# Queries and keys stored doubled and interleaved, loaded over 128 partitions; VectorE and GpSimd operations kept apart by the planner; down projection prepared five pairs ahead

## The chip, the cores and the metric

One core of a Trainium2 chip. The metric is the device time of one execution in microseconds (us); for the kernel before it is the median of three runs. PE is TensorE, DVE VectorE, ACT ScalarE, POOL GpSimd; SP issues DMAs, and so does ACT here.

## The reference

A decoder block on `x` of 1 x 1024 x 1024 in float32. One projection of the normed input gives a pooling branch, the queries and keys of four heads of differential attention, values and two gates; the gated sum of the two branches is projected and added, and a SwiGLU network of hidden width 2816 follows. Cut to what the change touches:

```python
z = einsum('bsd,de->bse', rms_norm(h, mix_pre_g), w_in)      # p, q, k, v, gate_a, gate_b
ya = einsum(pool_mixer(p), w_branch_a)
# 4 heads; each has two query halves and two key halves of width 64
a  = softmax(q1 k1' * scale + bias) - lam * softmax(q2 k2' * scale + bias)   # causal
yb = einsum(rms_norm(a @ v, subln_g) * (1 - lambda_init), w_branch_b)
m  = sigmoid(gate_a) * ya + sigmoid(gate_b) * yb
h  = h + rms_norm(m @ w_out, mix_post_g)
u  = rms_norm(h, ffn_pre_g)
f  = silu(u @ w_ffn_gate) * (u @ w_ffn_up)
h  = h + rms_norm(f @ w_ffn_down, ffn_post_g)
```

## The kernel before, in words

Every float32 operand is split into a high part (rounded to a shorter float32, type fp32r) and a low part (what is left), and a product of blocks is three matmuls: L799 (high by high), L800 and L801 (low by high, high by low). The large products run as units of seven half-size products (`seven_steps`, L824), accumulated in banks named Y, Z and X. In `seven_steps` the first product of a unit is copied out of Y by ACT (`p1`, L835), and the third product then goes on adding into the same bank Y; it can start only when that copy is done.

Stages by their time in the trace:
- 0 to 40 us: norm of the input and transposes.
- 40 to 112 us: queries and keys of the four heads. `qk_done` (L871) scales and splits each 128 x 512 result into a staging tile `qk_st` of high and low part and stores it into `qkd[h][e]` in device memory (e is 0 for queries, 1 for keys). The stores are issued on ACT's queue, by `store()` (L1040) for the first head and directly (L881) for the others.
- 112 to 327 us: values, pooling branch and gates. `load_head0` (L1192) loads head 0's tiles `K` and `QA` near the end.
- 327 to 527 us: `mixer` (L232), attention of 32 blocks of rows and both branch projections. Its order on every engine is written by a planner, the class `Plan` (L73): each step is a task with an engine, a cost, what it reads and writes and a rank; `schedule` (L142) runs a model of the engines, of the tile slots and of the DMA (`DMA_LATENCY`, `DMA_RATE`, L51) and fixes the order, which is emitted as it stands. At run time nothing of the planner's clock is left, only the order and the waits for data and for slots.
- 527 to 630 us: output projection (`out_matmul`, `out_norm`).
- 630 to 960 us: gate and up projections of the network; 960 to 1255 us: the down projection, L1430 to L1590. Outside the planned stages a general scheduler of the language arranges the engines' instructions.

In the mixer a head needs three tiles of 128 partitions x 2 x 1024. For each of the head's two maps m, `K` holds the key half's high part in one 64-partition half and its low part in the other; `QA` holds the query's high part in both halves and `QB` its low part in both halves. A score block is then two accumulated matmuls, `QA` by `K` and `QB` by `K`, and wants all three. The kernel before fills each tile with four DMAs of 64 partitions x 4 KB (256 KB each), so twelve for a head: `load_qk` (L343) issues those of `K` and `QA`, `load_bv` (L354) those of `QB` and then the one of the values `V`. SP issues all of them, in the planner's order (`dma`, L340).

The mixer's elementwise steps that matter here: `branch_weights` (L378) loads a 128 x 1024 weight block, casts it on ACT (L383) and forms the low part `wb_lo`, on POOL for the pooling branch (L385, weights against their high part) and on DVE for the attention branch (L655 by `k.sub`). `scores` (L423) ends with a scaled sum of the two maps (E, DVE, L465). `head_norm` (L516) computes 1/rms per row on POOL (`rstd`, a power, L522) and multiplies the head's output with it on DVE (`O` by `rstd`, issued by the helper `tt`, L257). The transposed attention block `AT` is split by ACT and DVE (low part at L655), and PE then multiplies it with `V`.

The down projection works through 77 pairs (a block of the hidden layer and a block of its weights): `load_s` (L1459) loads two pairs' worth of hidden blocks `s_raw`, `operands` (L1467) splits both into `s_op` and `w_op` on ACT (L732) and DVE (L655), `down_block` does 12 matmuls. The loop prepares pair n + DEPTH before the matmuls of pair n, and fetches `s_raw` of pair n + DEPTH + 3. In the last product, `residual` (L1510) loads the rows to be added (`hr`), and `finish` (L1515) adds and stores them.

## Time and profile before

| | us |
|---|---|
| median of three runs | 1266.66 |
| the three runs | 1263.72, 1266.66, 1266.82 |
| the profiled execution | 1262.81 |
| its span (first to last instruction) | 1261.0 |

The views used below come from the profiled execution; their times count from the span's start. A line of the waits says which engine, doing what, waited for whom, and then the total in us, how often, and the longest. A line of a timeline says start, duration, engine, line, operation, output and inputs, with the idle time before it and who ended that in brackets. A line of the windows says from:to, length, the busy time of each engine with its count, the clock that PE was granted (1.00 is full), the share of the DMA engines' time and the GB/s.

### The profile page before, as it was taken

How to read it: one execution, taken by the hardware profiler on the slowest of the kernel's cores; microseconds unless marked ns; L12 is line 12 of the kernel's file. 1: busy time of each engine (PE TensorE's matmuls, PEld its weight loads, DVE VectorE, ACT ScalarE, POOL GpSimd, SP SyncE). 2: the span in 40 equal slices, each digit the busy share in tenths (PEclk: the TensorE clock that was granted, in tenths of full speed). 3: DMA queues.
4: the chain of work that ended last, by engine and by line, in shares of the span. 5: the costliest groups of instructions: out<-in, count | busy, mean ns of one | idle time of the engine just before them, and what ended most of it. 6: DMA issues, size and time to landing. Idle time of an engine off the chain costs nothing.

```text
span 1261.0 us, 15705 instructions
## 1 busy us (share of the span) xinstructions
PE 1244.0 (99%) x5912; PEld 1042.4 (83%) x5912; DVE 837.3 (66%) x1296; ACT 581.2 (46%) x1039; POOL 144.0 (11%) x128
## 2 busy tenths in 40 slices
PE   8999999999999999999999999999999999999997
PEld 8888888888888998888888888888888888888886
DVE  5985785535589998755697645645645547965666
ACT  7553344434567874344553333333333333554542
POOL 4100000000201100010102111111111012000221
PEclk9999999999999999999999999999999999999999
DMA  8363338323797128423314332223322367733336
GB/s 254 114 192 131 136 123 246 112 92 117 242 272 186 52 69 283 150 101 118 117 59 126 125 107 102 92 94 108 125 100 96 115 212 276 244 102 100 90 94 209
DMA packets 135453, 179.15 MB, mean 142 GB/s; under 512 B 7633, under 2 KB 90321, under 8 KB 132945
## 3 DMA queue, kind: packets, MB, share of 16 engines
q1 hardware_dynamic: 124832, 147.61, 37.7%
q10 hardware_dynamic: 10544, 30.54, 6.3%
q8 instruction: 46, 0.75, 0.3%
q14 instruction: 31, 0.25, 0.1%
HBM read 124.39 MB, written 53.74 MB: 141 GB/s over the span
## 4 chain that ended last, share of the span: by engine, by line
PE 89%; DMA 3%; DVE 3%; issue 2%; ACT 1%; POOL 1%; SPq 0%; POOLq 0%; DVEq 0%; ACTq 0%
PE Y L799 10%; PE Y L800 10%; PE Y L801 10%; PE X L799 5%; PE X L801 5%; PE X L800 5%; PE Yd L800 3%; PE Z L801 3%; PE Z L800 3%; PE Yd L801 3%; PE Z L799 3%; PE Yd L799 3%; PE o L254 2%; PE branch L799 2%; PE branch L800 2%; PE branch L801 2%
## 5 line engine op out<-in xcount | busy, mean ns | idle before, releaser
L728 DVE TENSOR_TENSOR p<-Z,p 128x512 f32<-128x512 f32 x34 | 23.5, 691 | 162.8 <-PE Z L801 154.0
L800 PE MATMUL Y<-A_lo,Wh 128*128 128x512 f32 x296 | 115.4, 390 | 0.3 <-DVE A_lo L655 0.3
L799 PE MATMUL Y<-A_hi,Wh 128*128 128x512 f32 x296 | 115.3, 390 | 0.0
L801 PE MATMUL Y<-A_hi,Wl 128*128 128x512 f32 x296 | 115.2, 389 | 0.0
L799 PE MATMUL X<-S_hi,Wh 128*128 128x512 f32 x280 | 109.2, 390 | 0.0
L799 PE MATMUL Y<-S_hi,Wh 128*128 128x512 f32 x280 | 109.2, 390 | 0.0
L801 PE MATMUL Y<-S_hi,Wl 128*128 128x512 f32 x280 | 109.1, 389 | 0.0
L800 PE MATMUL Y<-S_lo,Wh 128*128 128x512 f32 x280 | 109.0, 389 | 0.0
L800 PE MATMUL X<-S_lo,Wh 128*128 128x512 f32 x280 | 108.9, 389 | 0.0
L801 PE MATMUL X<-S_hi,Wl 128*128 128x512 f32 x280 | 108.9, 389 | 0.0
L768 ACT CAST Wh<-wf_t 128x1024 fp32r<-128x1024 f32 x70 | 72.9, 1055 | 72.1 <-PE X L800 30.6
L768 ACT CAST Wh<-w_raw 128x1024 fp32r<-128x1024 f32 x72 | 60.7, 844 | 66.0 <-PE Z L800 39.9
L655 DVE TENSOR_TENSOR Wl<-wf_t,Wh 128x1024 fp32r<-128x1024 f32 x70 | 87.1, 1251 | 5.1 <-ACT Wh L768 5.1
L655 DVE TENSOR_TENSOR w_op<-wd,w_op 128x512 fp32r<-128x512 f32 x77 | 56.4, 732 | 49.8 <-ACT w_op L732 49.8
L732 ACT CAST w_op<-wd 128x512 fp32r<-128x512 f32 x77 | 48.0, 623 | 73.2 <-PE Yd L801 30.7
L655 DVE TENSOR_TENSOR Wl<-w_raw,Wh 128x1024 fp32r<-128x1024 f32 x72 | 69.1, 960 | 13.9 <-ACT Wh L768 13.9
L799 PE MATMUL Yd<-w_op,s_op 128*128 128x512 f32 x176 | 68.7, 390 | 0.6 <-ACT w_op L732 0.6
L800 PE MATMUL Yd<-w_op,s_op 128*128 128x512 f32 x176 | 68.7, 390 | 0.3 <-DVE w_op L655 0.3
L801 PE MATMUL Yd<-w_op,s_op 128*128 128x512 f32 x176 | 68.3, 389 | 0.0
L728 DVE TENSOR_TENSOR wf_t<-w_raw,wf_t 128x512 f32<-128x512 f32 x70 | 65.7, 939 | 1.1
L800 PEld LDWEIGHTS Y<-A_lo,Wh 128*128 128x128 f32 x296 | 55.6, 188 | 12.1 <-DVE A_lo L655 0.7
L801 PEld LDWEIGHTS Y<-A_hi,Wl 128*128 128x128 f32 x296 | 55.6, 188 | 11.6
(274 smaller groups left out, 3063.1 us busy)
## 6 DMA issues: line engine op xcount, KB each, us to landing
s_raw<-fsd SPq DMA_DIRECT2D x35, 512.0 KB, 3.6
w_raw<-in_w_in_dram SPq DMA_DIRECT2D x32, 512.0 KB, 4.2
w_raw<-in_w_ffn_gate_dram SPq DMA_DIRECT2D x22, 512.0 KB, 3.9
w_raw<-in_w_ffn_up_dram SPq DMA_DIRECT2D x22, 512.0 KB, 3.8
fsd<-fss SPq DMA_DIRECT2D x11, 1024.0 KB, 3.9
wd<-in_w_ffn_down_dram SPq DMA_DIRECT2D x44, 256.0 KB, 5.6
fsd<-F SPq DMA_DIRECT2D x33, 256.0 KB, 2.3
qkd<-qk_st ACTq DMA_DIRECT2D x16, 512.0 KB, 3.8
```

The source lines that it names most:

```text
L254: nc.tensor.matmul(o, l, r, start=start, stop=stop, skip_group_check=skip)
L655: nc.vector.tensor_tensor(out=o, in0=a, in1=f32(hi), op=ALU.subtract)
L728: nc.vector.tensor_tensor(out=o, in0=a, in1=b, op=op)
L732: nc.scalar.copy(hi, a)
L768: nc.scalar.copy(hi, a)
L799: nc.tensor.matmul(o, ah, bh, start=start, stop=False, skip_group_check=goes_on)
L800: nc.tensor.matmul(o, ah, bl, start=False, stop=False, skip_group_check=goes_on)
L801: nc.tensor.matmul(o, al, bh, start=False, stop=stop, skip_group_check=goes_on)
```

## The change

Three edits.

First, the stores and loads of queries and keys. Instead of `qkd[h][e]` there are `qd[h][i]` (i = 0 the high parts of the queries, 1 the low parts) and `kd[h]`. Of the queries, each part is written twice next to itself: a store of one part of `qk_st`, broadcast over two copies. Of the keys, high and low part lie side by side in each row, as before. Read as rows (partition, copy), 64 partitions of the store give 128 rows, so a load of half a tile covers all 128 partitions with one DMA of 512 KB. A head takes six loads for twelve; a result of a query takes two stores of 512 KB for one. The 128 rows now alternate between high and low part (`K`) in place of lying in two blocks; `QA` and `QB` hold equal rows in pairs, so the sum over the partitions is the same.

Second, the planner. Its tasks get a flag `port`. Flagged DVE tasks (the `wb_lo` and output-weight low parts, E, `O` by `rstd`, two steps of the gated sum) are not started in the model while a flagged POOL task (`wb_lo` at L385, `rstd` at L522) runs, and the other way round. No instruction is added; the emitted order may differ. The two DMA constants of the model are changed as well.

Third, `DEPTH` in the down projection is 5 in place of 3.

```diff
-DMA_LATENCY, DMA_RATE = 2.2, 0.36
+DMA_LATENCY, DMA_RATE = 2.4, 0.38
...
+        t.port = port
...
-                    at = max(f, ready, self.room(t))
+                    at = max(f, ready, self.room(t), port["POOL" if e == "DVE" else "DVE"] if t.port else 0.0)
...
+            if t.port:
+                port[e] = t.end
...
+def interleaved(src, m):
+    return src[m * HD:(m + 1) * HD].rearrange("p i s -> (p i) s")
...
         for m in range(2):
-            r, r2 = hs[m], hs[1 - m]
-            dma(lambda m=m, r=r: f32(K()[r, m, :]), lambda r=r: k.qkd[h][1][r, 0, :], rank, 0.262, w=[(K, (m, 0))])
-            dma(lambda m=m, r=r2: f32(K()[r, m, :]), lambda r=r: k.qkd[h][1][r, 1, :], rank, 0.262, w=[(K, (m, 1))])
-            for rr in (r, r2):
-                dma(lambda m=m, rr=rr: f32(QA()[rr, m, :]), lambda r=r: k.qkd[h][0][r, 0, :], rank, 0.262,
-                    w=[(QA, (m, rr.start))])
+            dma(lambda m=m: f32(K()[:, m, :]), lambda m=m: interleaved(k.kd[h], m), rank, 0.524, w=[(K, m)])
+            dma(lambda m=m: f32(QA()[:, m, :]), lambda m=m: interleaved(k.qd[h][0], m), rank, 0.524, w=[(QA, m)])
...
         for m in range(2):
-            for rr in hs:
-                dma(lambda m=m, rr=rr: f32(QB()[rr, m, :]), lambda m=m: k.qkd[h][0][hs[m], 1, :], rank, 0.262,
-                    w=[(QB, (m, rr.start))])
+            dma(lambda m=m: f32(QB()[:, m, :]), lambda m=m: interleaved(k.qd[h][1], m), rank, 0.524, w=[(QB, m)])
...
-              r=[ms], w=[r], rank=rank)
+              r=[ms], w=[r], rank=rank, port=True)
...
-    qkd = [[dr.tile([P, 2, S], F32, name=name("qkd")) for _ in range(2)] for _ in range(NH)]
+    qd = [[dr.tile([P, 2, S], F32, name=name("qd")) for _ in range(2)] for _ in range(NH)]
+    kd = [dr.tile([P, 2, S], F32, name=name("kd")) for _ in range(NH)]
...
-        if stores is None:
-            nc.scalar.dma_start(qkd[h][e][:, :, half(t)], f32(st))
+        if e == 1:
+            out_ = [(kd[h][:, :, half(t)], f32(st))]
         else:
-            stores.append((qkd[h][e][:, :, half(t)], f32(st)))
+            out_ = [(qd[h][i][:, :, half(t)], f32(st[:, i:i + 1, :]).to_broadcast([P, 2, HALF])) for i in range(2)]
+        if stores is not None:
+            stores.extend(out_)
+            return
+        for o, s in out_:
+            nc.scalar.dma_start(o, s)
...
-            nc.sync.dma_start(f32(K[r, m, :]), qkd[0][1][r, 0, :])
-            nc.sync.dma_start(f32(K[r2, m, :]), qkd[0][1][r, 1, :])
-            for rr in (r, r2):
-                nc.sync.dma_start(f32(QA[rr, m, :]), qkd[0][0][r, 0, :])
+            nc.sync.dma_start(f32(K[:, m, :]), interleaved(kd[0], m))
+            nc.sync.dma_start(f32(QA[:, m, :]), interleaved(qd[0][0], m))
...
-    kept, loaded, DEPTH, SPLIT = {}, {}, 3, 6
+    kept, loaded, DEPTH, SPLIT = {}, {}, 5, 6
```

The flag `port=True` is set in the same way on the other steps named above.

More of the change, by code (lines that the diff above doesn't have):

```diff
@@ L92, in given, with op @@
         return s
-    def op(self, engine, cost, fn, r=(), w=(), rank=0.0, size=0.0, claim=(), chain=None, behind=None):
+    def op(self, engine, cost, fn, r=(), w=(), rank=0.0, size=0.0, claim=(), chain=None, behind=None,
+           port=False):
         t = Task(engine, cost, fn, rank, size)
+        t.port = port
         if behind is not None:
@@ L146, in schedule @@
         open_ = {e: [] for e in free}
-        dma_free, order = 0.0, []
+        dma_free, order, port = 0.0, [], {"DVE": 0.0, "POOL": 0.0}
         for t in self.tasks:
@@ L363, in load_bv @@
         return QB, Vt
-    hs = [slice(0, HD), slice(HD, P)]
     seq = [(h, qb) for h in range(NH) for qb in (QLAST if h == NH - 1 else QORDER)]
@@ L385, in branch_weights @@
             pl.op("POOL", 2.6, lambda: G.tensor_tensor(out=lo(), in0=raw(), in1=f32(hi()), op=ALU.subtract),
-                  r=[raw, hi], w=[lo], rank=rank)
+                  r=[raw, hi], w=[lo], rank=rank, port=True)
         else:
-            pl.op("DVE", 1.23, lambda: k.sub(lo(), raw(), hi()), r=[raw, hi], w=[lo], rank=rank)
+            pl.op("DVE", 1.23, lambda: k.sub(lo(), raw(), hi()), r=[raw, hi], w=[lo], rank=rank, port=True)
         return hi, lo
@@ L466, in scores @@
                                                                     in1=view[0](), op0=ALU.mult, op1=ALU.add),
-              r=[E[1], cf], w=[E[0]], rank=r0 + .3)
+              r=[E[1], cf], w=[E[0]], rank=r0 + .3, port=True)
         attends[h, qb] = E[0], view[0], rec
@@ L527, in fn @@
             tt(o, o, r().unsqueeze(2).to_broadcast([P, n, P]), ALU.mult)
-        pl.op("DVE", dve(n * P), fn, r=[r], w=[(O[h], q) for q in blocks], rank=rank)
+        pl.op("DVE", dve(n * P), fn, r=[r], w=[(O[h], q) for q in blocks], rank=rank, port=True)
     def turn_head(h, t, rank):
@@ L580, in mixer @@
         pl.op("DVE", dve(HALF), lambda m=m, c=c, sg=sg: tt(m()[:, c, :], m()[:, c, :], sg()[:, 0], ALU.mult),
-              r=[(sg, 0)], w=[(m, c)], rank=r0 + 2)
+              r=[(sg, 0)], w=[(m, c)], rank=r0 + 2, port=True)
         if (1, d) in (k.unfinished if k else [(1, 6), (1, 7)]):
@@ L588, in mixer @@
         pl.op("DVE", dve(HALF), lambda m=m, c=c, sg=sg: tt(m()[:, c, :], m()[:, c, :], sg()[:, 1], ALU.add),
-              r=[(sg, 1)], w=[(m, c)], rank=r0 + 1)
+              r=[(sg, 1)], w=[(m, c)], rank=r0 + 1, port=True)
     wo = []
@@ L601, in mixer @@
             pl.op("DVE", 1.23, lambda hi=hi, lo=lo, j=j, raw=raw: k.sub(lo()[:, j, :], raw(), hi()[:, j, :]),
-                  r=[raw, (hi, j)], w=[(lo, j)], rank=rank)
+                  r=[raw, (hi, j)], w=[(lo, j)], rank=rank, port=True)
         wo.append((hi, lo))
@@ L1195, in load_head0 @@
         for m in range(2):
-            r, r2 = (slice(i * HD, (i + 1) * HD) for i in (m, 1 - m))
-            nc.sync.dma_start(f32(K[r, m, :]), qkd[0][1][r, 0, :])
-            nc.sync.dma_start(f32(K[r2, m, :]), qkd[0][1][r, 1, :])
-            for rr in (r, r2):
-                nc.sync.dma_start(f32(QA[rr, m, :]), qkd[0][0][r, 0, :])
+            nc.sync.dma_start(f32(K[:, m, :]), interleaved(kd[0], m))
+            nc.sync.dma_start(f32(QA[:, m, :]), interleaved(qd[0][0], m))
         return QA, K
@@ L1211, in block_kernel @@
         U=U, W=weights(*gate_cols(unfinished)), head0=head0, temp=temp, sub=sub, sumsq=sumsq, mhalf=mhalf, ident=ident,
-        nlam=nlam, sgc=sgc, qkd=qkd, vd=vd, yd=yd, sgd=sgd, unfinished=unfinished, w_branch_a=w_branch_a,
+        nlam=nlam, sgc=sgc, qd=qd, kd=kd, vd=vd, yd=yd, sgd=sgd, unfinished=unfinished, w_branch_a=w_branch_a,
         w_branch_b=w_branch_b, w_out=w_out))
```

## The prediction

> **What bounds the kernel now.** I read the page first, for what the end of the span depends on.

> ```profile
> span 1261.0 us, 15705 instructions
> PE 1244.0 (99%) x5912; PEld 1042.4 (83%) x5912; DVE 837.3 (66%) x1296; ACT 581.2 (46%) x1039; POOL 144.0 (11%) x128
> PE 89%; DMA 3%; DVE 3%; issue 2%; ACT 1%; POOL 1%; SPq 0%; POOLq 0%; DVEq 0%; ACTq 0%
> ```

> PE is busy for 1244.0 of 1261.0 us, and the chain that ended last runs through it for 89%. The change neither adds nor removes a matmul, so all that it can win is PE's idle 17.0 us, and whatever part of the 1244.0 ran at less than full clock. PE's waits say where the idle time lies.

> ```profile
> PE s L254 <- DMA QB<-qkd: 2.3, 1, 2.3
> PE x_t L945 <- DVE xt L917: 2.2, 2, 1.4
> PE k L935 <- POOL ident masks.py:199: 1.4, 1, 1.4
> PE o L254 <- DVE AT L655: 1.3, 1, 1.3
> PE q L675 <- DVE A_lo L655: 1.3, 2, 0.8
> ...
> PE Yd L799 <- ACT w_op L732: 0.6, 1, 0.6
> PE Yd L800 <- DVE w_op L655: 0.3, 1, 0.3
> ```

> The longest wait, 2.3 us, is for a QB load, on the first edit's path. The 1.3 us for AT lies in the planned mixer (second edit); the 0.6 and 0.3 us in the down projection (third). The others stand in the opening norm, which keeps its data and order but for one store issue. Then I cut PE and its clock in windows round the QB wait.

> ```profile
> 355.00:362.40 7.40, 7.40 (x46) 1.00 1.03 234
> 362.40:365.26 2.86, 0.54 (x3) 1.00 1.04 281
> 365.26:368.67 3.41, 3.41 (x10) 0.50 1.02 350
> 368.67:376.00 7.33, 7.33 (x47) 1.00 1.02 244
> ```

> After the gap PE runs at clock 0.50 for 3.41 us and executes 10 matmuls; it counts as busy there, so the list of waits doesn't show this second price.

> **First edit: loads.** When QB was issued, when PE wanted it, and how fast the loads went:

> ```profile
> 354.56 3.88 SPq L341 DMA_DIRECT2D QB<-qkd  x4
> 364.76 0.47 PE L254 MATMUL s<-K,QB 128*128 128x512 f32 x1 [2.33 <-DMA QB<-qkd]
> 336.00:353.60 17.60, 1.00 1.05 369
> 353.60:366.80 13.20, 0.94 1.02 258
> QB<-qkd SPq DMA_DIRECT2D x4, 256.0 KB, 8.9
> ```

> From 336.0 to 353.6 us the loads are of 128 partitions (pooling branch, values, weights): 369 GB/s. From 353.6 to 366.8 they are mostly head 1's twelve of 64 partitions: 258 GB/s, at the same full share of the DMA engines (1.05, 1.02). Twelve times 256 KB are 3.15 MB: 12.2 us at 258, 8.5 us at 369. The same bytes thus land about 3.7 us sooner, and QB at about 361.1 in place of 364.76, before the 362.43 at which PE began to wait. The 2.33 goes. What is late next is the next score block's tile, from the same six loads; it isn't waited for now and comes earlier too. Bounds: 0 if the new loads go at 258, -2.33 at most; I take -2.33, as 369 is measured on the shape that the new loads have. [...]

> With the gap goes, as I read it, the half-clock stretch: 3.41 us at half clock do 1.70 us of work, so -1.70 (0 to -1.70). For cause and effect speaks only that the stretch starts where the gap ends. [...]

> **First edit: stores.** The count and the cost on ACT:

> ```profile
> qkd<-qk_st ACTq DMA_DIRECT2D x16, 512.0 KB, 3.8
> 50.13 1.19 ACTq L1040 DMA_DIRECT2D qkd<-qk_st  x2
> 66.00:112.00 46.00, 46.00 (x204) 37.96 (x203) 35.62 (x49) 22.69 (x33) 2.88 (x3) 1.00 0.60 197
> ```

> There are 16 stores now, two for each of 4 heads and 2 halves, and 24 after: eight more issues on ACT at 0.6 us (1.19 for two), 4.8 us, and 4.2 MB more written. Six of the eight fall in the window from 66 to 112, where ACT is busy for 22.69 of 46.00: 3.6 us more leaves it two fifths idle. The DMA engines are at 0.60 and 197 GB/s there, so full they move about 328; 3.1 MB more are 9.6 us and bring 0.60 to 0.81. Nobody waits for the stores until head 0's loads, 200 us on. What queues behind each new issue on ACT are the weight casts and copies of the banks. At 50 us one more issue moves the next cast by 0.6:

> ```profile
> 50.61 2.28 DVE L655 TENSOR_TENSOR S_lo<-A_raw,S_hi 128x2048 fp32r<-128x2048 f32 x1
> 52.81 1.22 DVE L655 TENSOR_TENSOR Wl<-w_raw,Wh 128x1024 fp32r<-128x1024 f32 x1
> 51.37 1.06 ACT L768 CAST Wh<-w_raw 128x1024 fp32r<-128x1024 f32 x1 [1.42 <-DVE qk_st L655]
> ```

> That cast would end at 53.03 and not 52.43; DVE, which takes its result at 52.81 behind S_lo, starts 0.22 later. I book all this at 0; if the cover fails, up to 4.8 (rival B).

> One place does change. The general scheduler, given other instructions, interleaves the units otherwise: comparing the two orders, nine matmuls of the next unit stand before `Y<-S2` in the kernel before, and behind it after the change.

> ```profile
> 75.10 0.39 PE L801 MATMUL Y<-A_hi,Wl 128*128 128x512 f32 x1
> 75.33 0.39 PE L799 MATMUL Y<-A_hi,Wh 128*128 128x512 f32 x1
> 75.53 0.59 ACT L835 COPY p<-Y 128x512 f32<-128x512 f32 x1 [4.77 <-PE Y L801]
> 77.37 0.39 PE L799 MATMUL Y<-S_hi,Wh 128*128 128x512 f32 x1
> ```

> The unit's first product is issued by 75.10; from 75.33 to 77.37 PE now does the nine others, and ACT copies the bank meanwhile, 75.53 to 76.12. After the change PE comes to `Y<-S2` at 75.33 and waits for that copy: 76.12 less 75.33 are 0.79, with some handing over 0.86. PE takes its instructions in order, so all behind it waits too. Between 0 (other work slips in) and 1.5 (an issue of 0.6 ahead of the copy): +0.86.

> **Second edit: the planned order.** The timeline before the AT wait, and what the multiplication costs elsewhere:

> ```profile
> 391.38 2.40 POOL L385 TENSOR_TENSOR wb_lo<-wb_raw,wb_hi 128x1024 fp32r<-128x1024 f32 x1
> 391.53 3.34 DVE L257 TENSOR_TENSOR O<-O,rstd 128x1024 f32<-128x1024 f32 x1
> 394.79 1.15 DVE L655 TENSOR_TENSOR AT<-aT,AT 128x512 fp32r<-128x512 f32 x2
> 395.52 0.51 PE L254 MATMUL o<-V,AT 128*128 128x256 f32 x2 [1.32 <-DVE AT L655]
> L257 DVE TENSOR_TENSOR O<-O,rstd 128x1024 f32<-128x1024 f32 x3 | 5.8, 1923 | 0.0
> ```

> O by rstd takes 3.34 us here; three take 5.8 (1923 ns each, so 5.77), and the other two therefore 1.2 each. It began 0.15 us behind POOL's wb_lo, which ended at 393.78; 393.78 and 1.2 are 394.98, and it ended at 394.87. So DVE did nothing until POOL was done: 2.1 us lost, of which PE felt 1.32. [...] In the new order POOL does both wb_lo before that rstd, so this meeting doesn't occur: -1.32 (0 to -1.32).

> The order of the mixer is the same up to about 390 us and differs from there to 525. Where PE has no wait now but this one, a new order can only add: I put +0.4, between 0 and one wait like the old one, +1.32.

> **Third edit: DEPTH.** The instruction order of the down projection stays the same but for the last pairs, whose loads and casts come earlier.

> ```profile
> 1236.77 0.33 SPq L1463 DMA_DIRECT2D s_raw<-fsd  x1
> 1241.83 0.62 ACT L732 CAST s_op<-s_raw 128x512 fp32r<-128x512 f32 x1 [1.16 <-DMA s_raw<-fsd]
> 1243.02 0.49 PE L799 MATMUL Yd<-w_op,s_op 128*128 128x512 f32 x1 [0.60 <-ACT w_op L732]
> 1243.83 0.50 PE L800 MATMUL Yd<-w_op,s_op 128*128 128x512 f32 x1 [0.32 <-DVE w_op L655]
> ```

> The last s_raw is issued at 1236.77, ACT waits 1.16 for it, and PE then 0.60 and 0.32. Issued ahead of the `hr` loads it lands earlier, but ACT's casts now share the stretch with output stores: -0.5, of 0 to -0.92.

> **The sum.** -2.33 - 1.70 + 0.86 - 1.32 + 0.4 - 0.5 = -4.6 us. Against the profiled execution, 1262.81 us with its span of 1261.0: 1258.2, span 1256.4. The median of the three runs lies 3.85 above the profiled execution; on its scale the forecast is 1266.66 - 4.6 = **1262.1 us**.

> **Rivals.** [...] The edit delays the planner's own tasks; an operation held back still stands ahead of others on its engine. If the 1.32 comes back elsewhere, the sum is -3.3, 1263.4. For it: DVE has hardly any idle time, as the windows show.

> ```profile
> 390.00:410.00 20.00, 18.68 (x113) 16.18 (x112) 19.07 (x45) 15.03 (x45) 3.78 (x2) 1.00 0.78 184
> 410.00:430.00 20.00, 20.00 (x134) 18.47 (x133) 18.36 (x51) 16.60 (x46) 4.07 (x2) 1.00 0.17 54
> ```

> B: the eight issues aren't hidden on ACT. If four of them stand ahead of a copy or cast that PE awaits, 4 x 0.6 = 2.4 come back: -2.2, 1264.5. Against it: ACT's 22.69 of 46.00. [...]

> C: the clock stretch comes on its own: -2.9, 1263.8. [...]

> D, slower: holding DVE off POOL starves PE. In the 40 us from 390 to 430 DVE idles 0.93 + 1.64 = 2.57 and POOL works 3.78 + 4.07 = 7.85. If none of these may run beside DVE's flagged work and nothing else fills, DVE ends 5.28 late; PE waits that long, and, with two gaps like that at 362, two half-clock stretches add 3.4: +8.7. The rest of the sum without the AT and replanning terms is -3.67, so +5.0: 1271.7. It decides when the new order costs PE over 3.67; over 7.5 it shows as slower. [...]

> That the third edit does nothing is possible too, as the order hardly moves: -4.1, within the forecast.

> **How the numbers follow.** About 0.3% of the time, 3.8 us, can be told from no change: below 1262.86 is faster. Main case 0.64, A 0.11, B 0.09, C 0.04, D 0.12. The main case lies so near the bound that 0.08 of it is within; faster is 0.56, the same 0.08 + 0.11 + 0.09 + 0.04 = 0.32, slower 0.12. Low end: all gains full and no costs, -2.33 - 1.70 - 1.32 - 0.92 = -6.3, from the profiled execution's 1262.81: 1256.5. High end: no gain at all from the slowest run before, 1266.8, which holds A, B and C and leaves out D.

> **What would show it.** Right: no PE wait for QB near 362, clock 1.00 there, O by rstd at 1.2 us throughout, a wait of about 0.9 us before `Y<-S2` near 75. Wrong: a PE wait of over 2 us in 390 to 525, casts on ACT late behind stores in 40 to 112, or the QB loads still landing at 258 GB/s.

## The result, and the profile after

| | before | after |
|---|---|---|
| median | 1265.19 us (six runs, 1262.72 to 1267.27) | 1257.64 us (six runs, 1257.33 to 1257.89) |
| ratio, 95% interval | | 0.9942 [0.9926, 0.9957] |
| profiled execution, its span | 1262.81, 1261.0 | 1257.79, 1255.9 |

The change makes the kernel 0.4% to 0.7% faster: 7.5 us between the medians, 5.0 us between the two profiled executions. Two things are to be explained: where the 5 us come from, and why the medians lie further apart, with the runs before scattered over 4.6 us and those after over 0.6.

The chain's share by engine and PE's waits, of the kernel after:

```profile
span 1255.9 us, 15668 instructions
PE 94%; DVE 2%; ACT 1%; issue 1%; POOL 1%; DMA 1%; SPq 0%; POOLq 0%; DVEq 0%; ACTq 0%
```

```profile
PE x_t L952 <- DVE xt L924: 3.7, 3, 1.7
PE k L942 <- POOL ident masks.py:199: 1.4, 1, 1.4
PE q L676 <- DVE A_lo L656: 1.3, 2, 0.8
PE h_t L1403 <- DVE og L1397: 0.7, 1, 0.7
PE Y L800 <- ACT p L836: 0.7, 1, 0.7
PE o L262 <- DVE O L511: 0.5, 1, 0.5
PE Y L801 <- DVE A_lo L656: 0.3, 1, 0.3
```

The waits for QB, for AT and for the last pairs (Yd) are gone. New are 0.7 us for the copy `p`, before `Y<-S2`, and 0.5 us for O. The waits for x_t in the opening norm have grown by 1.5 us; the part on the prediction comes back to them. Lines after the first edit have moved by a few numbers (L799 is L800, L257 is L265). Next, PE in the same windows as before, then the DMA windows and the QB loads:

```profile
362.40:365.26 2.86, 2.86 (x19) 1.00 1.00 348
365.26:368.67 3.41, 3.41 (x24) 1.00 1.03 406
```

```profile
336.00:353.60 17.60, 1.00 1.03 403
353.60:366.80 13.20, 1.00 1.03 380
```

```profile
QB<-qd SPq DMA_DIRECT2D x4, 512.0 KB, 10.9
```

The second DMA window mixes head 1's loads with what comes behind them, so here is the stretch of head 1's own loads, from the landing of the load ahead of them to the landing of the last one, first in the kernel before, then after:

```profile
353.60:366.74 13.14, 0.94 1.03 258
351.60:359.30 7.70, 1.00 1.03 416
```

Where PE had done 3 matmuls in a gap and 10 at half clock it does 19 and 24, at clock 1.00. Head 1's 3.15 MB take 7.7 us where they took 13.1, which is 410 GB/s for 240, with the same share of the DMA engines (1.03). (The windows count packets by their start, so a little of the neighbours is in their GB/s.) The 10.9 us from issue to landing is longer than the 8.9 before because each load is issued earlier and waits behind others: the first half of QB is issued from 347.61 for 354.56 and has landed at 358.0 for 364.6.

Both traces have 5912 matmuls on PE, and the start of the n-th in each gives a ledger of lost and won time (where the two orders differ, from 75 to 118 and from 392 to 490 us, only the ends of the stretch are compared):

| stretch | after less before, us | forecast |
|---|---|---|
| opening norm, to 40 us | +0.44 | 0 |
| queries and keys, 40 to 132 us | +0.95 | +0.86 |
| round the QB load, 353 to 373 us | -4.16 | -4.03 |
| rest of the mixer | -0.63 | -0.92 |
| last pairs of the down projection | -1.80 | -0.5 |
| sum | -5.2 | -4.6 |

### The profile page after: what moved, and what is told of

Same layout as the page of the kernel before. It is cut to its first block, busy times and chain, and to the rows that moved or that the text cites. A ratio compares the mean times of both kernels' runs of the same rounds, so it can differ in the third digit from the quotient of the medians.

```text
span 1255.9 us, 15668 instructions
## 1 busy us (share of the span) xinstructions
PE 1240.8 (99%) x5912; PEld 1040.8 (83%) x5912; DVE 835.3 (67%) x1296; ACT 578.3 (46%) x1039; POOL 144.2 (11%) x128
## 4 chain that ended last, share of the span: by engine, by line
PE 94%; DVE 2%; ACT 1%; issue 1%; POOL 1%; DMA 1%; SPq 0%; POOLq 0%; DVEq 0%; ACTq 0%
PE Y L800 10%; PE Y L801 10%; PE Y L802 10%; PE X L800 5%; PE X L801 5%; PE X L802 5%; PE Yd L800 3%; PE Yd L802 3%; PE Yd L801 3%; PE s L262 3%; PE Z L801 3%; PE Z L802 3%; PE Z L800 3%; PE o L262 3%; PE branch L800 2%; PE branch L801 2%
## 5 line engine op out<-in xcount | busy, mean ns | idle before, releaser
L801 PE MATMUL Y<-A_lo,Wh 128*128 128x512 f32 x296 | 115.4, 390 | 0.3 <-DVE A_lo L656 0.3
L800 PE MATMUL Y<-A_hi,Wh 128*128 128x512 f32 x296 | 115.4, 390 | 0.0
L800 PE MATMUL Y<-S_hi,Wh 128*128 128x512 f32 x280 | 109.2, 390 | 0.7 <-ACT p L836 0.7
L800 PE MATMUL X<-S_hi,Wh 128*128 128x512 f32 x280 | 109.2, 390 | 0.0
L801 PE MATMUL Y<-S_lo,Wh 128*128 128x512 f32 x280 | 109.1, 389 | 0.0
L801 PE MATMUL X<-S_lo,Wh 128*128 128x512 f32 x280 | 108.9, 389 | 0.0
L800 PE MATMUL Yd<-w_op,s_op 128*128 128x512 f32 x176 | 68.6, 390 | 0.0
L801 PE MATMUL Yd<-w_op,s_op 128*128 128x512 f32 x176 | 68.5, 389 | 0.0
L801 PEld LDWEIGHTS Y<-A_lo,Wh 128*128 128x128 f32 x296 | 55.6, 188 | 12.1 <-DVE A_lo L656 0.7
L800 PEld LDWEIGHTS Y<-A_hi,Wh 128*128 128x128 f32 x296 | 55.6, 188 | 11.8 <-DVE p L729 0.3
## 6 DMA issues: line engine op xcount, KB each, us to landing
s_raw<-fsd SPq DMA_DIRECT2D x35, 512.0 KB, 3.6
w_raw<-in_w_in_dram SPq DMA_DIRECT2D x32, 512.0 KB, 4.1
w_raw<-in_w_ffn_gate_dram SPq DMA_DIRECT2D x22, 512.0 KB, 3.7
w_raw<-in_w_ffn_up_dram SPq DMA_DIRECT2D x22, 512.0 KB, 3.7
wd<-in_w_ffn_down_dram SPq DMA_DIRECT2D x44, 256.0 KB, 5.6
fsd<-F SPq DMA_DIRECT2D x33, 256.0 KB, 2.3
qd<-qk_st ACTq DMA_DIRECT2D x16, 512.0 KB, 4.0
```

The lines of the kernel that those rows point to most:

```text
L800: nc.tensor.matmul(o, ah, bh, start=start, stop=False, skip_group_check=goes_on)
L801: nc.tensor.matmul(o, ah, bl, start=False, stop=False, skip_group_check=goes_on)
```

## The experiments

Each edit was first made alone.

**loads_only**, the first edit without the others:

```diff
-DMA_LATENCY, DMA_RATE = 2.4, 0.38
+DMA_LATENCY, DMA_RATE = 2.2, 0.36
-              r=[ms], w=[r], rank=rank, port=True)
+              r=[ms], w=[r], rank=rank)
...
-    kept, loaded, DEPTH, SPLIT = {}, {}, 5, 6
+    kept, loaded, DEPTH, SPLIT = {}, {}, 3, 6
```

(against the kernel after)

> The kernel before with the first edit alone (stores and loads; planner constants, flags and DEPTH as before). Theory: this edit carries nearly all of the gain. Between the traces of before and after, PE's position fell by 4.2 us round the QB load and rose by 0.9 us near 75 us; so -3.3 us in the profiled execution, PE at clock 1.00 from 355 to 376 us, no wait for QB, a wait of 0.7 us before Y<-S2 near 75 us, and the 1.3 us AT wait and the 0.9 us at the end still there. The runs of before lie at two levels (three at 1262.7 to 1263.7, three at 1266.7 to 1267.3), those of after at one (1257.3 to 1257.9). Theory on the levels: they come with the QB wait, so this kernel's runs lie at one level, about 1259.5. Rival: the levels come from the meeting of POOL and DVE in the mixer or from the tail, and then this kernel still has two levels about 4 us apart.

Measured: 1258.88 us (1258.70 to 1259.21, five runs) against 1264.74 for the kernel before (27 runs, 1261.56 to 1268.27); ratio 0.9965 [0.9953, 0.9978]. Its ledger against before: 0.9 lost in the queries and keys, 4.1 won round the load, nothing in the rest of the mixer, and 1.0 won at the end though DEPTH is 3. So the tail varies by about 1 us without any change to it: the last `s_raw` took 5.0 us from issue to landing in the kernel before and 3.7 here; why is not shown. The runs lie within 0.5 us; and 27 runs of the kernel before show no two levels, as six had seemed to, but a broad scatter. That the scatter comes with the QB wait is supported; that it has two levels is refuted.

**planner_only**, the flags and constants on the kernel before:

```diff
-DMA_LATENCY, DMA_RATE = 2.2, 0.36
+DMA_LATENCY, DMA_RATE = 2.4, 0.38
-                    at = max(f, ready, self.room(t))
+                    at = max(f, ready, self.room(t), port["POOL" if e == "DVE" else "DVE"] if t.port else 0.0)
```

> The kernel before with the second edit alone (flags and planner constants). Theory: O by rstd takes 1.2 us everywhere, the 1.3 us AT wait is gone and other waits of up to 0.7 us take its place, so -0.6 us net as the ledger of the two traces has it in 390 to 525 us; the QB wait of 2.3 us and the half-clock stretch stay, and so do two levels 4 us apart. [...]

**depth_only**, one constant on the kernel before:

```diff
-    kept, loaded, DEPTH, SPLIT = {}, {}, 3, 6
+    kept, loaded, DEPTH, SPLIT = {}, {}, 5, 6
```

> The kernel before with DEPTH 5 alone. PE's order is unchanged. Theory by the ledger of the two traces: the waits for the last pairs go, -0.9 to -1.8 us in the profiled execution; two levels stay. Rival: nothing, as the loads were only three instructions earlier: 0.

Measured: planner_only 1263.91 us (1260.68 to 1265.69, 11 runs), ratio 0.9996 [0.9983, 1.0009], nothing that shows; depth_only 1262.01 (1260.28 to 1263.82, 11 runs), ratio 0.9984 [0.9974, 0.9994], a small gain. Both keep the QB wait and the scatter. Their traces catch other executions of it. PE's waits, then its windows, in planner_only:

```profile
PE s L258 <- DMA QB<-qkd: 4.2, 1, 4.2
...
PE o L258 <- DVE O L514: 0.5, 1, 0.5
```

```profile
362.69:366.60 3.91, 0.00 (x0) 1.00 1.04 270
366.60:370.00 3.40, 3.11 (x8) 0.50 1.00 322
```

The same two views of depth_only:

```profile
PE s L254 <- DMA QB<-qkd: 3.2, 1, 3.2
...
PE o L254 <- DVE AT L655: 1.3, 1, 1.3
```

```profile
362.90:365.30 2.40, 0.00 (x0) 1.00 1.05 258
365.30:372.10 6.80, 6.00 (x18) 0.50 1.01 301
```

In planner_only the wait is 4.2 us, and PE is busy for 3.11 at half clock, which loses 1.55: 5.8 together. In depth_only it is 3.2, and 6.00 at half clock, which loses 3.0: 6.2. In the profiled execution of before the same place cost 2.33 + 1.70 = 4.0. In the ledger planner_only wins 0.55 in the rest of the mixer: AT's wait is gone and one of 0.5 for O has come. depth_only wins 1.80 at the end, all of it, with no wait for Yd left.

**late_qb**: is the half clock a consequence of the gap? The kernel after, with a gap put back by copies that nobody needs:

```diff
+            def src(m=m):
+                if h == 1 and m == 0:
+                    for n in range(3):
+                        nc.sync.dma_start(k.spare[n], k.vd[h])
+                return interleaved(k.qd[h][1], m)
-            dma(lambda m=m: f32(QB()[:, m, :]), lambda m=m: interleaved(k.qd[h][1], m), rank, 0.524, w=[(QB, m)])
+            dma(lambda m=m: f32(QB()[:, m, :]), src, rank, 0.524, w=[(QB, m)])
```

> The changed kernel with three added copies of 1 MB between tiles of device memory (head 1's stored values to unused tiles), issued on SP directly ahead of head 1's first QB load; the order of all else is the same. In the kernel after, that load lands at 358.0 us and PE needs it about 363.2. If the copies move 1 MB in 2.7 us as the loads do, QB lands about 8 us later and PE waits about 2.9 us. Theory (the gap halves the clock, and the levels come with it): a half-clock stretch of 3.4 us follows, 1.7 us lost in it, the profiled time rises by 4.6 us, and the runs spread over two levels. Rival (the half clock has another cause): the time rises by the wait alone, 2.9 us, with clock 1.00 behind it, and one level.

**gap_small** (the first copy is half as large; the first diff, against late_qb), **gap_big** (four copies; the second), and late_qb once more:

```diff
-                        nc.sync.dma_start(k.spare[n], k.vd[h])
+                        c = slice(0, S if n else HALF)
+                        nc.sync.dma_start(k.spare[n][:, :, c], k.vd[h][:, :, c])
```

```diff
-                    for n in range(3):
+                    for n in range(4):
```

> As late_qb, with the three copies cut to 0.5, 1 and 1 MB. In late_qb the wait was 2.79 us and its eleven runs fell into two groups, six at 1259.8 to 1260.1 and five at 1261.3 to 1262.1, 1.6 us apart; the profiled run was one of the upper group and shows one half-clock stretch of 3.4 us, which costs 1.7. Theory (the clock is judged in stretches of 3.4 us whose phase doesn't follow the program, so a gap shorter than one draws a half-clock stretch only in some executions): wait about 1.3 us, a half-clock stretch in few executions or none, one group near 1257.6 + 1.5 = 1259.1. Rival (any wait for a load halves the clock): two groups or one upper group, 1.7 us higher.

> As late_qb, with four copies of 1 MB. Wait about 5.7 us. Theory (phase): a gap longer than 3.4 us always draws at least one half-clock stretch, so no run without it: 1257.6 + 5.9 + 1.7 = 1265.2, or less where the half clock falls partly into the gap itself, and at most one further level above. Rival (the stretch comes by chance, whatever the gap): again a lower group, at 1263.5, with about half of the runs.

> The kernel of late_qb once more, for the trace of another execution. Theory: if its time is near 1260.0, its trace shows the same wait of about 2.8 us and clock 1.00 behind it; if it is near 1261.6, a half-clock stretch of 3.4 us. Rival: the two groups come from the length of the wait (about 1.6 us apart) with a half-clock stretch in both.

Measured: late_qb 1260.11 us (11 runs: six from 1259.76 to 1260.11, five from 1261.32 to 1262.07); gap_small 1260.25 (seven runs: five from 1259.24 to 1260.53, two at 1261.74 and 1261.85); gap_big 1265.09 (11 runs, 1264.36 to 1266.23); late_qb_again 1261.66. PE's windows of late_qb, gap_small and gap_big, in this order:

```profile
363.59:366.38 2.79, 0.00 (x0) 1.00 1.05 355
366.38:367.40 1.02, 1.02 (x6) 0.98 0.98 345
367.40:370.80 3.40, 3.40 (x11) 0.51 1.04 367
```

```profile
363.46:365.68 2.22, 0.00 (x0) 1.00 1.02 395
365.68:376.00 10.32, 10.32 (x61) 1.00 1.02 402
```

```profile
363.46:365.40 1.94, 0.00 (x1) 1.00 0.30 106
365.40:372.20 6.80, 3.31 (x9) 0.50 0.98 348
```

The gap makes the half clock: the kernel after has neither, late_qb has both. In the ledger late_qb loses 4.64 us more than the kernel after round the load (4.6 were expected), gap_small 2.50. But a gap of 2.22 us (gap_small, a miss: 1.3 was expected) drew no half-clock stretch in its profiled execution, where before's 2.33 drew one; so its length alone doesn't decide. late_qb_again was an execution of the upper group (2.70 us, then 3.40 at half clock).

No trace of late_qb's lower group was taken, but each run's mean granted clock over its span is on record. In the profiled executions it is 0.999 in all eight without a half-clock stretch behind a gap, 0.997 or 0.998 in the four with one stretch of 3.4 us, and 0.996 in the two with two (depth_only, gap_big). All six runs of late_qb's lower group have 0.999, the five of the upper group 0.997 or 0.998. So the lower group ran without the stretch, and the rival of late_qb_again, a stretch in both groups, is refuted. (One stretch loses 1.7 of 1260 us, 0.0014. A value of 0.998 alone doesn't tell: four runs of versions without the gap have it too.) split_rows below shows a gap of 2.42 us without a stretch in a trace. gap_big always pays: no run lies near 1263.5, where its wait alone would put it, and all eleven have 0.996 or 0.997. In the kernel before, the five of the 27 runs with 0.999 are the five fastest (1261.56 to 1262.36): the half clock is part of its scatter, and the length of the wait is likely the rest.

**sp_stores**: the wait near 75 us. The stores of `qk_done`'s direct place go to SP's queue:

```diff
         for o, s in out_:
-            nc.scalar.dma_start(o, s)
+            nc.sync.dma_start(o, s)
```

> The changed kernel with the query and key stores of heads 1 (its second issue place) to 3 issued on SP in place of ACT. In PE's order seven matmuls of the next unit stand between the unit's first product and Y<-S2 again, as nine did before. Theory (the wait near 75 us comes from that order, and the copy is the only thing late): the 0.9 us that PE lost near 75 us come back, 1257.64 - 0.9 = 1256.7. Rival (ACT's stores themselves or the added bytes hold PE up): no change near 75 us. Second rival: SP holds weight loads behind stores that wait for their data, and PE waits for weights in 75 to 112 us: slower than 1257.6.

> The changed kernel itself, beside the next one on the same chip. About 1257.6, with 0.9 us lost near 75 us.

> The kernel of sp_stores once more, beside the changed kernel on the same chip. Theory: 0.9 to 1.0 us faster than the changed kernel, 1256.7, with runs that don't overlap its runs. Rival (the chip of that call was the cause): the same time as the changed kernel.

Measured: sp_stores 1256.68 us (1256.43 to 1257.47, five runs), ratio to before 0.9938 [0.9926, 0.9951]. On one chip, after_again 1257.54 (1257.42 to 1258.22, four runs) and sp_stores_again 1256.41 (1256.32 to 1256.59, four runs), without overlap: 1.1 us faster than the changed kernel, and the fastest version here. The copy and the matmul behind it, first in the kernel after, then in sp_stores:

```profile
75.53 0.39 PE L802 MATMUL Y<-A_hi,Wl 128*128 128x512 f32 x1
75.96 0.58 ACT L836 COPY p<-Y 128x512 f32<-128x512 f32 x1 [4.67 <-PE Y L802]
76.60 0.50 PE L800 MATMUL Y<-S_hi,Wh 128*128 128x512 f32 x1 [0.68 <-ACT p L836]
```

```profile
76.35 0.57 ACT L836 COPY p<-Y 128x512 f32<-128x512 f32 x1
77.01 0.47 PE L800 MATMUL Y<-S_hi,Wh 128*128 128x512 f32 x1
```

ACT had idled for 4.67 us before the copy: no store stood in its way, the loss came from PE's order alone. In sp_stores the seven other matmuls stand between, and PE waits for nothing there. The stores write the same bytes, so these don't slow PE either; nor do weights come late behind them on SP.

**split_cols and split_rows**: is it the partitions, or the size and number of the loads? Every 512 KB load of the kernel after becomes two of 256 KB, by columns in split_cols (first) and by partitions in split_rows (second):

```diff
-        pl.op("SP", 0.38, lambda: nc.sync.dma_start(o(), i()), r=r, w=w, rank=rank, size=mb, behind=behind)
+            dst, src = o(), i()
+            for c in range(2):
+                nc.sync.dma_start(dst[:, c * HALF:(c + 1) * HALF], src[:, c * HALF:(c + 1) * HALF])
```

```diff
+                nc.sync.dma_start(dst[c * HD:(c + 1) * HD, :], src[c * HD:(c + 1) * HD, :])
```

> The changed kernel with each 512 KB load of K, QA and QB (heads 1 to 3, and QB of head 0) issued as two DMAs of 256 KB over 128 partitions, half of the columns each; all else in the same order. Theory (the number of partitions sets the rate): head 1's loads go at about 380 GB/s as in the kernel after, QB lands before 360 us, no wait, 1257.6. Rival (twelve smaller DMAs in place of six are what was slow): about 250 GB/s from 354 to 367 us, a wait for QB of 1 us or more, runs spread over more than 2 us.

> The changed kernel with the same loads issued as two DMAs of 256 KB over 64 partitions each, the shape of the kernel before, from the new stores. Theory (partitions): about 250 GB/s, QB lands at about 363 to 366 us, a wait of 0 to 3 us round 363, in some executions a half-clock stretch, runs spread over 3 us or more with a median near 1262. Rival (the layout in device memory or the size, not the partitions): as the kernel after, or as split_cols.

Measured: split_cols 1257.19 us (1257.02 to 1257.36, four runs), split_rows 1261.23 (1259.46 to 1263.09, ten runs). The DMA window of head 1's loads and the QB loads in split_cols:

```profile
352.90:360.70 7.80, 1.00 1.04 344
QB<-qd SPq DMA_DIRECT2D x4, 256.0 KB, 5.2
```

The same in split_rows, with PE's first matmul on QB and the window behind it:

```profile
354.70:367.70 13.00, 1.00 1.03 271
QB<-qd SPq DMA_DIRECT2D x4, 256.0 KB, 8.8
365.83 0.47 PE L262 MATMUL s<-K,QB 128*128 128x512 f32 x1 [2.42 <-DMA QB<-qd]
365.83:376.00 10.17, 10.17 (x59) 1.00 1.03 305
```

Twelve loads of 256 KB take 7.8 us over 128 partitions and 13.1 over 64, by their landings, or 402 and 240 GB/s (the windows' 344 and 271 again have neighbours in them). Size, number and the new layout in device memory are the same in both, and the pieces of a row are shorter in the faster one (2 KB for 4 KB), so it is the partitions. split_rows has the wait back, and the scatter: 3.6 us, where split_cols has 0.3. In this execution the gap of 2.42 us drew no half clock.

## Why the prediction was right, and where it was off

The direction and the range held: 1257.64 lies between 1256.5 and 1266.8, and faster had the largest chance. Step by step:

- QB wait and half clock: -4.03 forecast, -4.16 in the ledger. The forecast's rates, 258 and 369 GB/s, were those of windows with other loads in them; by the landings head 1's loads went from 240 to 410, so the first half of QB landed at 358.0 and not at 361.1. The sum didn't suffer, since any landing before 362.4 ends the wait. Rival C, a clock stretch of other origin, is refuted by late_qb and by the kernel after. The gap that drew the stretch was 2.33 us long, shorter than the stretch's 3.41; the last section has the others beside it.
- Wait for the p1 copy: +0.86 forecast, 0.68 as idle time and 0.95 in the ledger. The reason given, PE's order, is confirmed by sp_stores.
- Stores at 0: right. Rival B is refuted: the ledger loses nothing between 78 and 132 us. The DMA engines' share in the window from 66 to 112 us rose from 0.60 to 0.74, short of the 0.81 worked out.
- Planner: -1.32 and +0.4 forecast, -0.63 measured. The first O by rstd takes 3.33 or 3.34 us in the three traces with the old order and 1.22 in all others, as this group of the kernel after shows (two of the five work on half as many elements):

```profile
L265 DVE TENSOR_TENSOR O<-O,rstd 128x1024 f32<-128x1024 f32 (+1 forms) x5 | 5.0, 1006 | 0.0
```

  planner_only, with 0.55, says the same: the meeting is avoided, and a new wait of 0.5 us for O takes back about half. The term for replanning was too small: +0.4 forecast, about +0.7 measured. Rival A (the 1.32 comes back elsewhere) is thus half right, as about half of it did; D's 8.7 is refuted. One reading was off: POOL does one wb_lo ahead of that rstd, not both (386.95 to 389.36; the next starts at 412.88). What matters held: POOL does nothing while O by rstd runs, from 391.96. How POOL's wb_lo holds that multiplication up when the two meet, no run here shows.
- DEPTH: -0.5 of 0 to -0.92 forecast, -1.80 measured, outside its own bounds. Two errors. The last s_raw is issued at 1229.38 where it was 1236.77, which is 4.0 us more than PE's own 3.4, and lands at 1232.17 for 1241.81, far enough ahead that every wait goes. And the bound was a sum of idle times, while a wait cost PE more than that here: in this tail before, matmuls start 0.23 us apart and are drawn 0.39 long, so 0.16 of each wait is hidden behind the drawn end, and the matmul after it is drawn 0.50 long and takes 0.11 more. Five slow steps between starts add up to 1.77 us before, and to 0 after. How much there was to win is partly luck: with DEPTH still 3 the same tail cost 0.8 us in loads_only and 2.0 in planner_only.
- The opening norm's +0.44 isn't the change's: loads_only has -0.05 there and depth_only -0.01, sp_stores, with nearly the changed kernel's instructions, +0.1, and planner_only, with the old ones, +0.24. It follows the landing of the input's second block: 8.26 us in the kernel after (+0.44) and 8.30 in after_again (+0.49), 7.80 before, 8.07 in planner_only. The waits for x_t grew by more than that because PE was granted full clock earlier (from 4.40 for 6.86 us) and so came to the same input sooner.
- The scale: here the step failed that moved the sum from the profiled execution (1262.81) to the median of three runs (1266.66). The sum itself gave 1258.2, 0.4 us from the profiled 1257.79 (errors of +0.44, +0.29, -1.30 and smaller ones partly cancel in it). The 3.85 us between execution and median were taken to stay, and they did not. Part was the luck of three runs: 27 others of the kernel before have a median of 1264.74. The rest was part of what the change removes: the profiled execution had a cheap pass of the QB wait (4.0 us); others cost 5.8 and 6.2, and in the versions without that wait the runs lie within 0.3 to 1.0 us. So the median fell by 7.5 us where 4.6 were forecast. That the range held is luck in part: its low end, 1256.5, was counted from the profiled execution. From the median the same 6.3 us of gains give 1260.4, and the measured 1257.64 lies below that.

## What to carry to other kernels

Scatter between runs of a kernel on one core can itself be a cost with an address: here a wait that varied with a transfer (2.33, 3.20 and 4.20 us in three traces with the old loads), and a clock that fell to 0.50 behind it. Size such a term by several executions, and don't carry the distance between a profiled execution and the median over to a kernel from which that wait is gone. Loads that filled half of the partitions were worth a second copy in device memory, as PE waited for them: 3.15 MB took 13.1 us over 64 partitions and 7.7 over 128. And after moving DMA issues between queues, look at what the scheduler then does with PE's order.
